# Sixteen blocks of the down projections as seven products, with left operands made in the up phase

## The chip, the cores and the metric

One core of a Trainium2 chip runs the kernel. The time is that of one execution on the device, in microseconds (us); of several executions the median counts.

## What is computed

One decoder layer on x (1024 tokens, 1024 channels, float32): a feed-forward block, a mixer, a second feed-forward block. The change is in the two feed-forward blocks (FFN1 and FFN2), which have D_FF = 2816 channels:

```python
def swiglu(x, w_gate, w_up, w_down):
    return (jax.nn.silu(x @ w_gate) * (x @ w_up)) @ w_down
...
        f = swiglu(rmsnorm(x, ffn1_pre_g[l]), ffn1_w_gate[l], ffn1_w_up[l], ffn1_w_down[l])
        x = x + 0.5 * rmsnorm(f, ffn1_post_g[l])
```

## The kernel before

Every float32 product is made of three matmuls on high and low parts, `mm3` (L118 to L121: high x high, high x low, low x high), each 128 x 128 x 512. A high part is a rounded copy, a low part is the original minus it. The 2816 channels are 22 blocks `f` of 128. Tokens are 8 tiles `tt` of 128 or 2 halves `h` of 512.

**Up phase** (`Ffn.up`, L395). For each block, gate and up projection. Blocks 0 and 1 are plain; blocks 2 to 21 use a block form in which seven products of quarter matrices, combined with additions, stand for eight (`product`, L368). Products go in the order 1, 2, 5, 6, 4, 7, 3 into the PSUM banks X, Z, DY, DW; ACT copies partial sums out of a bank that a later product accumulates over (L374, L378, L382), DVE adds the rest (L383 to L390). `prep` (L291) makes the weights' operands for the next block: four DVE combinations (L297 to L300), seven high parts (four on POOL, L307; three on ACT, L305), seven low parts on POOL (L308). The operands are 512 elements wide; `slot` (L280) takes them from pool `fu` or `WP`, two halves to a tile. SP loads the weights two blocks ahead (`load`, L270). The block's result h goes to DRAM by ACT's queue (`put`, L347).

**Down phase** (`ffn_down`, L420). Blocks in four chunks `CH` of 6, 6, 6 and 4. For each chunk, output half n and token tile tt: SP loads h of the chunk from DRAM (L431), ACT makes the high part (L433), DVE the low part (L435), PE runs 3 matmuls for each block, ACT copies the bank (L452, first chunk) or DVE adds it to the sum `acc` (L454). Weights come 2 blocks x 512 columns at a time through `weight` (L93): SP loads 512 KB, POOL makes high and low part (L107, L108). After the last chunk `post` normalises and adds the residual.

Each engine runs its instructions in one fixed order, the order of the program text (SP's, ACT's and POOL's transfers included); a transfer waits in its engine's queue like any instruction. Pools of tiles with a fixed number of buffers decide how far an engine runs ahead.

## Time and profile before

| | us |
|---|---|
| median of 3 runs | 2267.06 (2266.55 to 2268.98) |
| profiled execution, whole time | 2267.87 |
| its span | 2266.1 |
| TensorE busy in it | 2142.8 (95%) |
| FFN1: up products, down | about 106 to 487, 487 to 737 |
| FFN2: up products, down | about 1630 to 2009, 2013 to 2258 |

The span is the time from the first to the last instruction; 1.77 us of the profiled execution lie outside it. The granted clock of the profiled execution is 0.97 on the mean. Rows of the profile name engine (PE is TensorE, DVE VectorE, ACT ScalarE, POOL GpSimd, SP the queue that issues most transfers), line, operation, output tile and input tiles, and shape.

### The profile page before, as it was taken

The page shows a single profiled execution, that of the slowest core. Times are in us where ns is not written, and L with a number is a line of the kernel's source. Part 1 is how long each engine was busy: PE and PEld are TensorE (multiplying, and loading weights), DVE is VectorE, ACT ScalarE, POOL GpSimd, SP SyncE. Part 2 cuts the span into 40 slices and gives each one's busy share as a digit, 9 for nine tenths or more (in the row PEclk, how much of TensorE's full clock was granted, in tenths as well). Part 3 has the DMA queues.
Part 4 walks back from the last instruction along what each step waited for, and adds up shares of the span by engine and source line. Part 5 has one row for each costly group of instructions (what it writes and reads, how often), then busy time and mean ns, then how long its engine had stood idle before and what let it go on. Part 6 is the DMA issues. An engine that isn't in the chain of part 4 may idle for free.

```text
span 2266.1 us, 29554 instructions
## 1 busy us (share of the span) xinstructions
PE 2142.8 (95%) x11168; PEld 1764.5 (78%) x11168; DVE 1102.3 (49%) x1652; ACT 786.0 (35%) x1349; POOL 963.7 (43%) x875
## 2 busy tenths in 40 slices
PE   7799999999999999999999999899799999999998
PEld 5678888878887777777888887777678888878886
DVE  4743333322445555735617778636743333322446
...
GB/s 116 70 93 91 75 90 75 67 142 183 142 149 130 93 164 119 109 168 99 229 161 117 187 200 108 130 139 121 76 91 84 84 84 84 66 137 169 130 135 162
DMA packets 295277, 276.16 MB, mean 122 GB/s; under 512 B 29664, under 2 KB 237536, under 8 KB 295136
## 3 DMA queue, kind: packets, MB, share of 16 engines
...
q14 instruction: 53, 0.43, 0.1%
HBM read 195.60 MB, written 78.64 MB: 121 GB/s over the span
## 4 chain that ended last, share of the span: by engine, by line
PE 78%; DVE 10%; POOL 4%; ACT 4%; issue 3%; DMA 1%; SPq 0%; DVEq 0%; ACTq 0%; POOLq 0%
PE f1d L120 3%; PE f1d L121 3%; PE f1d L119 3%; PE pj L119 3%; PE f2d L119 3%; PE f2d L120 3%; PE f2d L121 3%; PE pj L121 3%; PE pj L120 3%; PE f2X L119 2%; PE f2X L120 2%; PE f2X L121 2%; PE f1X L119 2%; PE f1X L121 2%; PE f1X L120 2%
## 5 line engine op out<-in xcount | busy, mean ns | idle before, releaser
L107 POOL TENSOR_SCALAR wh<-wr 128x1024 fp32r<-128x1024 f32 x87 | 112.1, 1289 | 480.3 <-PE f1d L121 152.8
L108 POOL TENSOR_TENSOR wl<-wr,wh 128x1024 fp32r<-128x1024 f32 x87 | 213.5, 2455 | 6.0 <-PE pj L121 0.2
L120 PE MATMUL f1d<-wl,f1hh 128*128 128x512 f32 x352 | 138.8, 394 | 3.9 <-POOL wl L108 3.9
L119 PE MATMUL f2d<-wh,f2hh 128*128 128x512 f32 x352 | 137.9, 392 | 4.7 <-issue 3.5
L121 PE MATMUL f1d<-wh,f1hl 128*128 128x512 f32 x352 | 138.6, 394 | 0.4 <-DVE f1hl L435 0.4
L119 PE MATMUL f1d<-wh,f1hh 128*128 128x512 f32 x352 | 138.1, 393 | 0.0
L120 PE MATMUL f2d<-wl,f2hh 128*128 128x512 f32 x352 | 137.7, 391 | 0.0
L121 PE MATMUL f2d<-wh,f2hl 128*128 128x512 f32 x352 | 137.4, 390 | 0.0
L308 POOL TENSOR_TENSOR f2wl<-f2S,f2wh 128x512 fp32r<-128x512 f32 x80 | 104.0, 1311 | 4.0 <-ACT f2wh L305 1.7
L308 POOL TENSOR_TENSOR f1wl<-f1S,f1wh 128x512 fp32r<-128x512 f32 x80 | 103.9, 1310 | 4.0 <-ACT f1wh L305 1.7
L433 ACT CAST f2hh<-f2r 128x768 fp32r<-128x768 f32 (+1 forms) x56 | 45.1, 808 | 165.8 <-PE f2d L120 109.1
L433 ACT CAST f1hh<-f1r 128x768 fp32r<-128x768 f32 (+1 forms) x56 | 45.1, 807 | 165.7 <-PE f1d L120 109.8
L435 DVE TENSOR_TENSOR f2hl<-f2r,f2hh 128x768 fp32r<-128x768 f32 (+1 forms) x56 | 55.8, 998 | 68.9 <-ACT f2hh L433 68.9
L435 DVE TENSOR_TENSOR f1hl<-f1r,f1hh 128x768 fp32r<-128x768 f32 (+1 forms) x56 | 56.5, 1008 | 66.5 <-ACT f1hh L433 66.5
L308 POOL TENSOR_TENSOR f2wl<-f2r,f2wh 128x512 fp32r<-128x512 f32 x60 | 86.0, 1440 | 2.3
L308 POOL TENSOR_TENSOR f1wl<-f1r,f1wh 128x512 fp32r<-128x512 f32 x60 | 85.9, 1439 | 2.3
L307 POOL TENSOR_SCALAR f1wh<-f1r 128x512 fp32r<-128x512 f32 x40 | 33.4, 837 | 114.8 <-DMA f1r<-in_ffn_w_gate_dram 60.3
L119 PEld LDWEIGHTS f2d<-wh,f2hh 128*128 128x128 f32 x352 | 66.4, 189 | 19.6 <-issue 3.9
L120 PEld LDWEIGHTS f1d<-wl,f1hh 128*128 128x128 f32 x352 | 66.9, 190 | 18.5 <-POOL wl L108 4.7
L121 PEld LDWEIGHTS f1d<-wh,f1hl 128*128 128x128 f32 x352 | 66.9, 190 | 14.7 <-DVE f1hl L435 0.8
L119 PEld LDWEIGHTS f1d<-wh,f1hh 128*128 128x128 f32 x352 | 66.8, 190 | 14.0
L307 POOL TENSOR_SCALAR f2wh<-f2r 128x512 fp32r<-128x512 f32 x40 | 33.4, 835 | 104.0 <-DMA f2r<-in_ffn_w_gate_dram 49.5
...
## 6 DMA issues: line engine op xcount, KB each, us to landing
wr<-in_ffn_w_down_dram SPq DMA_DIRECT2D x44, 512.0 KB, 3.9
f1r<-f1h_d SPq DMA_DIRECT2D x48, 384.0 KB, 3.5
f2r<-f2h_d SPq DMA_DIRECT2D x48, 384.0 KB, 3.5
wr<-in_w_in_dram SPq DMA_DIRECT2D x27, 512.0 KB, 4.0
f1r<-in_ffn_w_gate_dram SPq DMA_DIRECT2D x20, 512.0 KB, 3.9
f1r<-in_ffn_w_up_dram SPq DMA_DIRECT2D x20, 512.0 KB, 4.0
f2r<-in_ffn_w_gate_dram SPq DMA_DIRECT2D x20, 512.0 KB, 3.9
f2r<-in_ffn_w_up_dram SPq DMA_DIRECT2D x20, 512.0 KB, 3.9
```

The costliest lines, as they stand in the source:

```text
L107: nc.gpsimd.tensor_scalar(wh, raw, 1.0, 0.0, op0=ALU.mult, op1=ALU.add)
L108: nc.gpsimd.tensor_tensor(wl, raw, wh, op=ALU.subtract)
L119: nc.tensor.matmul(ps, lhsT=lh, rhs=rh, start=first, stop=False, **kw)
L120: nc.tensor.matmul(ps, lhsT=lh, rhs=rl, start=False, stop=False, **kw)
L121: nc.tensor.matmul(ps, lhsT=ll, rhs=rh, start=False, stop=last, **kw)
L307: nc.gpsimd.tensor_scalar(wh, src[n], 1.0, 0.0, op0=ALU.mult, op1=ALU.add)
L308: nc.gpsimd.tensor_tensor(wl, src[n], wh, op=ALU.subtract)
L433: nc.scalar.copy(hh, raw)
L435: nc.vector.tensor_tensor(hl, raw, hh, op=ALU.subtract)
```

## The change

The up phase now also makes the down projection's left operands. `split_pair` takes two neighbouring blocks' h (`hv`), makes the seven combinations that the block form needs, splits each into high (ACT) and low (DVE), and stores both with SP (256 KB each); its seven pieces are called by `split_step` between the matmul groups of the next even block's `product`. The plain blocks 0, 1 and 18 to 21 are split without combining. The results are in three DRAM tiles `hf` (blocks 0, 1), `hs` (2 to 17) and `hl` (18 to 21). The pools of the up phase change: S 2 to 1 tiles, wh and wl 2 to 1, tp 8 to 6, new are hv 2 and st 6.

The down phase starts with blocks 0 and 1 (plain, six matmuls per bank), goes on with four groups `c` of four blocks in the seven-product form, each with 4 steps `i` of two token tiles (42 matmuls, seven additions by DVE), and ends with blocks 18 to 21 (plain). `prep(c + 1)` stands at the first step of group c: four weight loads, four DVE combinations (128x1024), seven high parts on ACT, seven low parts on POOL. Left operands come from DRAM ready to use, once.

```diff
-    CH = [(0, 6), (6, 6), (12, 6), (18, 4)]
+    NS, FS, FL = 4, 2, 18
...
+            self.hf = dr.tile([NT, P, 2, 2, P], F32, name=f"{nm}hf_d")
+            self.hs = dr.tile([NS, 4, 8, P, 2, 2, P], F32, name=f"{nm}hs_d")
+            self.hl = dr.tile([NT, 2, P, 4, P], F32, name=f"{nm}hl_d")
...
-                pool = self.fu if i % 6 < 2 else WP
+                pool = self.fu if i % 5 < 1 else WP
...
             src = {1: A11, 2: A12, 5: S1, 6: S2, 4: A22, 7: S3, 3: S4}
             for n in PO:
+                if n == 3:
+                    tt(S4, A12, S2, op=ALU.subtract)
                 wh, wl = self.slot()
...
+            t = WP.tile("wr", f"{self.nm}es{f}_{h}", [P, 1024], F32R)
+            self.split(hv, t[:, 0:HT], t[:, HT:], lambda x: self.hf[4 * h:4 * h + 4, :, x, f, :])
...
+        def split(self, src, hi, lo, dst):
+            nc.scalar.copy(hi, src)
+            nc.vector.tensor_tensor(lo, src, hi, op=ALU.subtract)
+            for x, t in enumerate((hi, lo)):
+                nc.sync.dma_start(dst(x).rearrange("i p t -> p i t"),
+                                  t.bitcast(F32).rearrange("p (i t) -> p i t", t=P))
...
+        def split_pair(self, f):
+            v = [self.hv.pop(x).rearrange("p (i b t) -> p b i t", b=2, t=P) for x in (f, f + 1)]
+            A11, A21, A12, A22 = v[0][:, 0], v[0][:, 1], v[1][:, 0], v[1][:, 1]
+            c, k = divmod(f - FS, 4)
+            v3 = lambda t: t.rearrange("p (i t) -> p i t", t=P)
+            tt = nc.vector.tensor_tensor
+            def out_(n, src):
+                hi, lo = self.st("sh"), self.st("sl")
+                nc.scalar.copy(v3(hi), src)
+                tt(v3(lo), src, v3(hi), op=ALU.subtract)
+                for x, t in enumerate((hi, lo)):
+                    nc.sync.dma_start(self.hs[c, :, n, :, x, k // 2, :].rearrange("i p t -> p i t"),
+                                      v3(t.bitcast(F32)))
+            out_(1, A11)
+            yield
+            out_(2, A12)
+            yield
+            s1 = v3(self.st("s1", F32))
+            tt(s1, A21, A22, op=ALU.add)
+            out_(5, s1)
+            yield
+            s2 = v3(self.st("s2", F32))
+            tt(s2, s1, A11, op=ALU.subtract)
+            out_(6, s2)
+            yield
+            out_(4, A22)
+            yield
+            tt(s1, A11, A21, op=ALU.subtract)
+            out_(7, s1)
+            yield
+            tt(s2, A12, s2, op=ALU.subtract)
+            out_(3, s2)
...
         def product(self, f):
             self.mm(f, 1, "X")
+            self.split_step()
             self.mm(f, 2, "Z")
+            self.split_step()
             self.evac1(f)
             y = self.mm(f, 5, "DY")
             y5 = self.tile(f, "y")
             nc.scalar.copy(y5, y)
-            self.store(f - 1)
+            self.split_step()
             x = self.mm(f, 6, "X", False)
             u2 = self.tile(f, "u")
             nc.scalar.copy(u2, x)
+            self.split_step()
             w = self.mm(f, 4, "DW")
+            self.split_step()
...
+            h = self.hv[f] = self.fu.tile("hv", f"{self.nm}hv{f}", [P, T])
+            nc.vector.tensor_tensor(h[:, 0:HT], p1, u3, op=ALU.mult)
+            nc.vector.tensor_tensor(h[:, HT:T], u2, y5, op=ALU.mult)
+            if f >= FL:
+                self.sp.append(self.split_plain(f))
+            elif (f - FS) % 2:
+                self.sp.append(self.split_pair(f - 1))
...
-            self.fu = Pool(self.nm + "u", dict(raw=2, S=2, wh=2, wl=2, tp=8))
+            self.fu = Pool(self.nm + "u", dict(raw=2, S=1, wh=1, wl=1, tp=6, hv=2, st=6))
...
+        rp = Pool(nm + "rp", dict(wh=6, wl=6, rw=5, T=2), "right")
...
+        def slot():
+            i = nslot[0]
+            nslot[0] += 1
+            pool = rp if i % 10 < 6 else WP
+            return [v2(pool.tile(t, f"{nm}d{t}{i}", [P, 1024], F32R)) for t in ("wh", "wl")]
+        def prep(c):
+            f0 = FS + 4 * c
+            first = slot()
+            B = {}
+            for kh, e in ((0, 0), (0, 1), (1, 1), (1, 0)):
+                B[kh, e] = v2(rp.tile("rw", f"{nm}B{c}{kh}{e}", [P, 1024]))
+                nc.sync.dma_start(B[kh, e], F.wd[:, f0 + kh:f0 + kh + 4:2, e * 512:(e + 1) * 512])
+            T1, T2 = [v2(rp.tile("T", f"{nm}T{c}{i}", [P, 1024])) for i in range(2)]
+            tt = nc.vector.tensor_tensor
+            tt(T1, B[0, 1], B[0, 0], op=ALU.subtract)
+            tt(T2, B[1, 1], T1, op=ALU.subtract)
+            src = {1: B[0, 0], 2: B[1, 0], 5: T1, 6: T2, 3: B[1, 1], 7: B[0, 1], 4: B[1, 0]}
+            for n in (1, 2, 5, 6, 3, 7, 4):
+                if n == 7:
+                    tt(B[0, 1], B[1, 1], B[0, 1], op=ALU.subtract)
+                if n == 4:
+                    tt(B[1, 0], B[1, 0], T2, op=ALU.subtract)
+                wh, wl = first or slot()
+                first = None
+                nc.scalar.copy(wh, src[n])
+                nc.gpsimd.tensor_tensor(wl, src[n], wh, op=ALU.subtract)
+                op[c, n] = wh, wl
...
+        W = [weight(F.wd[:, 0:2, n * 512:(n + 1) * 512], 2, 512, False) for n in range(2)]
+        prep(0)
+        for tt in range(NT):
+            h2 = pl.tile("ho", f"{nm}hf{tt}", [P, 2, 2, P], F32R)
+            nc.sync.dma_start(h2.bitcast(F32), F.hf[tt])
+            for n in range(2):
+                ps = bank("A", f"{nm}df{n}_{tt}")
+                for i in range(2):
+                    mm3(ps, h2[:, 0, i, :], h2[:, 1, i, :], W[n][0][:, i, :], W[n][1][:, i, :], i == 0, i == 1)
+                nc.scalar.copy(quarter(tt, n), ps)
...
+        for s_, (c, i) in enumerate(steps):
+            if i == 0 and c + 1 < NS:
+                prep(c + 1)
+            if s_ + 1 < len(steps):
+                hos[steps[s_ + 1]] = hload(*steps[s_ + 1])
+            ho = hos.pop((c, i))
+            a_, b_ = 2 * i, 2 * i + 1
+            X = bank("A", f"{nm}dX{c}{i}")
+            mm(c, ho, 1, X, True)
+            add(a_, 0, X)
+            if late is not None:
+                late()
+            Z = bank("D", f"{nm}dZ{c}{i}")
+            mm(c, ho, 2, Z, True)
+            add(a_, 0, Z)
+            Y = bank("mm", f"{nm}dY{c}{i}")
+            mm(c, ho, 5, Y, True)
+            add(b_, 1, Y)
+            mm(c, ho, 6, X, False)
+            add(a_, 1, X)
+            mm(c, ho, 3, Y, False)
+            add(a_, 1, Y)
+            mm(c, ho, 7, X, False)
+            add(b_, 1, X)
+            def late(c=c, ho=ho, X=X, b_=b_):
+                mm(c, ho, 4, X, False)
+                add(b_, 0, X)
```

Three places in the order of the engines follow. The first is ACT in the up phase at block 8 of FFN1, in the kernel before: `p8`, `y8`, `u8`, `v8` are copies of banks, `wh` weight operands.

```order
L357 COPY f1p8_1568<-f1X8_1542 128x512
L305 CAST f1wh_27_1532<-f1S9_1_1513 128x512
L359 ACTIVATE f1p8_1568<-f1p8_1568 128x512
L374 COPY f1y8_1585<-f1DY8_1572 128x512
L305 CAST f1wh_28_1654<-f1r0_10_1538 128x512
L378 COPY f1u8_1601<-f1X8_1542 128x512
L305 CAST f1wh_29_1660<-f1S10_0_1648 128x512
L382 COPY f1v8_1628<-f1X8_1542 128x512
L387 ACTIVATE f1u8_1601<-f1u8_1601 128x512
```

After it stands:

```order
L451 ACTIVATE f1u7_1564<-f1u7_1564 128x512
L382 CAST f1sh35_1673<-f1hv7_1609 128x512
L421 COPY f1p8_1679<-f1X8_1641 128x512
L382 CAST f1sh38_1700<-f1s137_1698 128x512
L311 CAST f1wh_26_1624<-f1S9_1612 128x512
L423 ACTIVATE f1p8_1679<-f1p8_1679 128x512
L382 CAST f1sh41_1722<-f1s240_1720 128x512
L434 COPY f1y8_1696<-f1DY8_1683 128x512
L382 CAST f1sh43_1741<-f1hv7_1609 128x512
L382 CAST f1sh45_1764<-f1s137_1698 128x512
L311 CAST f1wh_27_1630<-f1r1_9_1505 128x512
L438 COPY f1u8_1718<-f1X8_1641 128x512
```

The casts of L382 (`sh`, the high parts of the combinations of blocks 6 and 7) stand among the copies; between `p8` and `u8` there are four of them.

The second is SP at the end of the up phase of FFN1, before (`wr` down weights, `r0` the chunk's h, the operand of the first down matmuls):

```order
L276 DMA f1r1_21_3048<-in_ffn1_w_up_dram 128x8x128
L104 DMA wr4_3418<-in_ffn1_w_down_dram 128x2x512
L104 DMA wr5_3424<-in_ffn1_w_down_dram 128x2x512
L104 DMA wr6_3430<-in_ffn1_w_down_dram 128x2x512
L104 DMA wr7_3652<-in_ffn1_w_down_dram 128x2x512
L431 DMA f1r0_0_3412<-f1h_d0_120 128x768
```

And after (`ph`, `pl` the parts of block 21's h; `B` weights of the first seven-product group; `hf0` the left operand of the first down matmuls):

```order
L513 DMA f1B000_3838<-in_ffn1_w_down_dram 128x2x512
L359 DMA f1hl_d_122<-f1ph141_3791 128x4x128
L359 DMA f1hl_d_122<-f1pl142_3792 128x4x128
L359 DMA f1hl_d_122<-f1ph143_3797 128x4x128
L359 DMA f1hl_d_122<-f1pl144_3798 128x4x128
L513 DMA f1B001_3840<-in_ffn1_w_down_dram 128x2x512
L513 DMA f1B011_3842<-in_ffn1_w_down_dram 128x2x512
L513 DMA f1B010_3844<-in_ffn1_w_down_dram 128x2x512
L542 DMA f1hf0_3878<-f1hf_d_120 128x512
L542 DMA f1hf1_3896<-f1hf_d_120 128x512
```

The loads of h stand behind the stores of block 21 and three more loads of weights.

The third is DVE in FFN1's down phase, before, in the second chunk (`f1hl` low parts of h, `f1d` banks):

```order
L454 TENSOR_TENSOR f1acc0_3455<-f1d1_0_0_3896,f1acc0_3455 128x512
L435 TENSOR_TENSOR f1hl1_3_3972<-f1r1_3_3968,f1hh1_3_3970 128x768
L454 TENSOR_TENSOR f1acc1_3482<-f1d1_0_1_3922,f1acc1_3482 128x512
L435 TENSOR_TENSOR f1hl1_4_3998<-f1r1_4_3994,f1hh1_4_3996 128x768
L454 TENSOR_TENSOR f1acc2_3509<-f1d1_0_2_3948,f1acc2_3509 128x512
L435 TENSOR_TENSOR f1hl1_5_4024<-f1r1_5_4020,f1hh1_5_4022 128x768
```

After, where the first step of group 1 begins (`dX03` and `dY03` are banks of the last step of group 0, `dX10`, `dZ10`, `dY10` of this one; `T2` and `B2` are combinations for group 2):

```order
L499 TENSOR_TENSOR f1acc6_3819<-f1dY03_4306,f1acc6_3819 128x512
L499 TENSOR_TENSOR f1acc7_3820<-f1dX03_4283,f1acc7_3820 128x512
L517 TENSOR_TENSOR f1T21_4346<-f1B211_4341,f1T20_4345 128x1024
L521 TENSOR_TENSOR f1B201_4339<-f1B211_4341,f1B201_4339 128x1024
L499 TENSOR_TENSOR f1acc0_3813<-f1dX10_4391,f1acc0_3813 128x512
L499 TENSOR_TENSOR f1acc7_3820<-f1dX03_4283,f1acc7_3820 128x512
L523 TENSOR_TENSOR f1B210_4343<-f1B210_4343,f1T21_4346 128x1024
L499 TENSOR_TENSOR f1acc0_3813<-f1dZ10_4406,f1acc0_3813 128x512
L499 TENSOR_TENSOR f1acc1_3814<-f1dY10_4414,f1acc1_3814 128x512
```

Three combinations for the next group but one stand before the addition that empties `dY10`.

## Rows read from the trace of the kernel before

**Rows 1.** The page: busy time by engine, and the chain that ended last.
```profile
PE 2142.8 (95%) x11168; PEld 1764.5 (78%) x11168; DVE 1102.3 (49%) x1652; ACT 786.0 (35%) x1349; POOL 963.7 (43%) x875
...
PE 78%; DVE 10%; POOL 4%; ACT 4%; issue 3%; DMA 1%; SPq 0%; DVEq 0%; ACTq 0%; POOLq 0%
```

**Rows 2.** Two stretches: busy us (instructions) of PE, PEld, DVE, ACT, POOL; clock, DMA, GB/s.
```profile
130.00:480.00 350.00, 348.24 (x1537) 288.03 (x1536) 131.08 (x180) 97.09 (x165) 209.62 (x195) 1.00 0.29 82
480.00:500.00 20.00, 17.59 (x70) 13.64 (x69) 8.20 (x9) 4.91 (x8) 11.46 (x6) 0.91 0.63 198
```

**Rows 3.** The page's costliest groups: busy, mean ns, idle before.
```profile
L108 POOL TENSOR_TENSOR wl<-wr,wh 128x1024 fp32r<-128x1024 f32 x87 | 213.5, 2455 | 6.0 <-PE pj L121 0.2
L120 PE MATMUL f1d<-wl,f1hh 128*128 128x512 f32 x352 | 138.8, 394 | 3.9 <-POOL wl L108 3.9
```

**Rows 4.** Timeline, POOL and DVE, 287 to 291 us: start, length, instruction, [idle before].
```profile
287.02 1.29 POOL L308 TENSOR_TENSOR f1wl<-f1S,f1wh 128x512 fp32r<-128x512 f32 x1
288.27 1.29 POOL L308 TENSOR_TENSOR f1wl<-f1r,f1wh 128x512 fp32r<-128x512 f32 x1
...
288.34 1.76 DVE L299 TENSOR_TENSOR f1S<-f1r,f1r 128x512 f32<-128x512 f32 x1 [4.29 <-POOL f1wl L308]
```

**Rows 5.** Groups by line and shape, 130 to 480 us, POOL, DVE and ACT.
```profile
L308 POOL TENSOR_TENSOR f1wl<-f1S,f1wh 128x512 fp32r<-128x512 f32 x70 | 90.4, 1301 | 3.9 <-ACT f1wh L305 1.7
L307 POOL TENSOR_SCALAR f1wh<-f1S 128x512 fp32r<-128x512 f32 x35 | 21.9, 627 | 64.9 <-PE f1Z L120 19.1 <-PE f1X L120 17.4 <-PE f1DW L120 14.9
...
L390 DVE TENSOR_TENSOR f1y<-f1u,f1y 128x512 f32<-128x512 f32 x19 | 17.5, 919 | 1.4 <-ACT f1u L387 1.4
...
L305 ACT CAST f1wh<-f1S 128x512 fp32r<-128x512 f32 x35 | 21.8, 623 | 58.6 <-PE f1X L120 34.8 <-PE f1DY L120 17.7 <-PE f1X L121 3.4
L378 ACT COPY f1u<-f1X 128x512 f32<-128x512 f32 x19 | 11.1, 586 | 22.0 <-PE f1X L121 22.0
```

**Rows 6.** Timeline, POOL, at the start of FFN1's up products.
```profile
85.67 7.43 POOL L307 TENSOR_SCALAR f1wh<-f1r 128x512 fp32r<-128x512 f32 x1 [60.34 <-DMA f1r<-in_ffn_w_gate_dram]
```

**Rows 7.** Timeline, PE and DVE, from FFN1's last up matmul on.
```profile
486.87 0.39 PE L121 MATMUL f1DY<-X_1h,f1wl 128*128 128x512 f32 x1
487.10 0.39 PE L119 MATMUL f1d<-wh,f1hh 128*128 128x512 f32 x1
...
489.51 0.50 PE L121 MATMUL f1d<-wh,f1hl 128*128 128x512 f32 x1 [0.42 <-DVE f1hl L435]
...
493.17 0.50 PE L120 MATMUL f1d<-wl,f1hh 128*128 128x512 f32 x1 [1.99 <-POOL wl L108]
...
495.46 0.63 PE L119 MATMUL f1d<-wh,f1hh 128*128 128x512 f32 x1
495.89 0.63 PE L120 MATMUL f1d<-wl,f1hh 128*128 128x512 f32 x1
...
487.30 0.69 DVE L386 TENSOR_TENSOR f1u<-f1DY,f1u 128x512 f32<-128x512 f32 x1
...
489.37 1.53 DVE L390 TENSOR_TENSOR f1y<-f1u,f1y 128x512 f32<-128x512 f32 x1
```

**Rows 8.** Timeline, PE, from FFN2's last up matmul on.
```profile
2008.90 0.39 PE L121 MATMUL f2DY<-x2X4h,f2wl 128*128 128x512 f32 x1
2012.83 0.47 PE L119 MATMUL f2d<-wh,f2hh 128*128 128x512 f32 x1 [3.54 <-issue]
```

**Rows 9.** DMA issues: count, KB each, median us to landing.
```profile
wr<-in_ffn_w_down_dram SPq DMA_DIRECT2D x44, 512.0 KB, 3.9
f1r<-f1h_d SPq DMA_DIRECT2D x48, 384.0 KB, 3.5
...
f1r<-f1h_d SPq DMA_DIRECT2D x8, 256.0 KB, 2.6
```

**Rows 10.** Groups by line and shape, DVE, 500 to 730 us.
```profile
L454 DVE TENSOR_TENSOR f1acc<-f1d,f1acc 128x512 f32<-128x512 f32 x45 | 31.0, 690 | 71.8 <-PE f1d L121 71.5
L496 DVE TENSOR_TENSOR f1acc<-f1acc,gpost 128x1024 f32<-128x1024 f32 x5 | 6.1, 1220 | 1.3 <-ACT x1q0j L480 0.7 <-ACT x1q1j L480 0.6
```

More of the change, by code (lines that the diff above doesn't have):

```diff
@@ L292, in prep @@
             G, U = self.raw.pop(f)
-            S = [self.fu.tile("S", f"{self.nm}S{f}_{i}", [P, 1024]) for i in range(2)]
-            S1, S2, S3, S4 = [self.half(S[i // 2], i % 2) for i in range(4)]
+            S = self.fu.tile("S", f"{self.nm}S{f}", [P, 1024])
+            S1, S2 = [self.half(S, i) for i in range(2)]
             A11, A12, A21, A22 = G[:, 0:4], G[:, 4:8], U[:, 0:4], U[:, 4:8]
+            S3, S4 = A21, A12
             tt = nc.vector.tensor_tensor
@@ new lines, in split_plain @@
+        def split_plain(self, f):
+            t = self.hv.pop(f)
+            for h in range(2):
+                self.split(t[:, h * HT:(h + 1) * HT], self.st("ph"), self.st("pl"),
+                           lambda x: self.hl[4 * h:4 * h + 4, x, :, f - FL, :])
+                yield
[28 more added lines that the diff above has]
+            out_(7, s1)
+            yield
+            tt(s2, A12, s2, op=ALU.subtract)
+            out_(3, s2)
@@ L352, in tile, with split_step @@
+        def split_step(self):
+            while self.sp:
+                try:
+                    next(self.sp[0])
+                    return
+                except StopIteration:
+                    self.sp.pop(0)
         def tile(self, f, n):
@@ L360, in evac1 @@
             self.tp[f] = p1
-        def store(self, f):
-            if f not in self.tp:
-                return
-            for h, t in enumerate(self.tp.pop(f)):
-                self.put(f, h, t)
         def product(self, f):
             self.mm(f, 1, "X")
+            self.split_step()
             self.mm(f, 2, "Z")
+            self.split_step()
             self.evac1(f)
@@ L416, in up, with ffn_down @@
                 self.product(f)
[L417 removed]
+            while self.sp:
+                self.split_step()
             self.fu.close()
[L420 removed]
+    def ffn_down(pl, F, gb, post, half=None, nextx=None):
         nm = F.nm
[L422 to L469 removed]
@@ new lines, in ffn_down, with add @@
+        acc = [pl.t4(f"{nm}acc{tt}") for tt in range(NT)]
+        rp = Pool(nm + "rp", dict(wh=6, wl=6, rw=5, T=2), "right")
+        quarter = lambda tt, n: acc[tt][:, n * 512:(n + 1) * 512]
+        v2 = lambda t: t.rearrange("p (k e) -> p k e", k=2)
+        nslot = [0]
+        op = {}
+        def add(tt, n, ps):
+            nc.vector.tensor_tensor(quarter(tt, n), ps, quarter(tt, n), op=ALU.add)
+        def slot():
[3 more added lines that the diff above has]
+            return [v2(pool.tile(t, f"{nm}d{t}{i}", [P, 1024], F32R)) for t in ("wh", "wl")]
@@ new lines, in ffn_down, with mm @@
+        steps = [(c, i) for c in range(NS) for i in range(4)]
+        hos = {steps[0]: hload(*steps[0])}
+        late = None
+        def mm(c, ho, n, ps, first):
+            wh, wl = op[c, n]
+            for k in range(2):
+                mm3(ps, ho[n][:, 0, k, :], ho[n][:, 1, k, :], wh[:, k, :], wl[:, k, :], first and k == 0, k == 1,
+                    skip_group_check=True)
+        for s_, (c, i) in enumerate(steps):
[25 more added lines that the diff above has]
+                add(b_, 0, X)
@@ new lines, in ffn_down @@
+        late()
+        rp.close()
+        if nextx is not None:
+            nextx()
+        ex = EX[0] = Pool(nm + "ex", dict(wh=2, wl=2), "right")
+        gb[0] = gb[0]()
+        W = {}
+        for tt in range(NT):
+            hh, hl = [pl.tile("ho", f"{nm}hl{x}{tt}", [P, 4, P], F32R) for x in range(2)]
+            for x, t in enumerate((hh, hl)):
+                nc.sync.dma_start(t.bitcast(F32), F.hl[tt, x])
+            for n in range(2):
+                ps = bank("A", f"{nm}dl{n}_{tt}")
+                for i in range(4):
+                    if (n, i // 2) not in W:
+                        W[n, i // 2] = weight(F.wd[:, FL + i:FL + i + 2, n * 512:(n + 1) * 512], 2, 512, i == 2)
+                    dh, dl = W[n, i // 2]
+                    mm3(ps, hh[:, i, :], hl[:, i, :], dh[:, i % 2, :], dl[:, i % 2, :], i == 0, i == 3)
+                add(tt, n, ps)
+                if half is not None and tt == NT - 1:
+                    half(n, acc[tt])
+            if half is None or tt < NT - 1:
+                post(tt, acc[tt])
@@ L1390, in layer_kernel @@
     PS.open("psf2d", FP)
-    HP = Pool("h2", HB, "right")
-    pl = EX[0] = Pool("f2", dict(FB, t4=20, t2=4))
+    pl = Pool("f2", dict(FB, t2=4))
     gb = [lambda: bcast(pl, "gpost2", a["ffn2_post_g"], 0.5)]
-    ffn_down(pl, HP, F2, gb, *make_last(pl, "x3", x2_d, gb, out[0]))
+    ffn_down(pl, F2, gb, *make_last(pl, "x3", x2_d, gb, out[0]))
     pl.close()
-    HP.close()
     WP.close()
```

85 lines of the change are left out of this document (20 added, 65 removed).

## The prediction

> **What bounds the kernel now.** I read the share of busy time and the chain of waits first: TensorE is busy 2142.8 of the 2266.1 us span and carries 78% of the chain [rows 1]. Then the stretches, to see where that is literally so. From 130 to 480 us, the seven-product part of the first FFN's up phase, PE is busy 348.24 of 350 us at full granted clock while POOL is busy only 209.62 and DVE 131.08 [rows 2]. The second FFN runs the same code. The down projection between 500 and 736 us is as dense, apart from a few waits on POOL's low parts of weights. So a removed matmul is worth its full slot, and each new wait of PE costs its full length. In the profile PE idles round the FFNs only at three places: the start of the up products, the hand-over from up to down, and the last chunk's first weights. The question for this change is whether the engines off the path stay off it, because it gives DVE, ACT and SP more to do and takes buffers from POOL.
>
> **1. Matmuls removed.** One down projection is 22 blocks x 8 token tiles x 2 halves x 3 = 1056 matmuls, 352 by each of three lines [rows 3]. Sixteen blocks in seven products instead of eight leave 4 groups x 4 token pairs x 42 = 672, and six plain blocks 288: 960, so 96 fewer per FFN and 192 in all. A slot is 348.24 / 1537 = 0.2266 us [rows 2]. 192 x 0.2266 = **-43.5 us** over both FFNs, with nothing else in its way. A product of six matmuls lasts 1.36 us and a step of 42 lasts 9.52; an up product of 84 lasts 19.04.
>
> **2. The up phase gets work on DVE, ACT and SP.** The split of h moves here from the down phase. Every second block (f = 4, 6 ... 18: eight per FFN) now carries seven casts on ACT, eleven 128x512 operations on DVE and fourteen stores on SP; I call it a heavy block. ACT has room: 97 of 350 us [rows 2], and seven casts of 0.62 more in 19 us. DVE looks idle as well (37%), but it does not run freely beside POOL. At 288.34 the add of L299 had waited 4.29 us for POOL and then took 1.76 us instead of 0.69, and it finished only when POOL's two subtractions of 1.29 us were done [rows 4]. L390 averages 0.919 over the stretch for the same reason [rows 5]. So for DVE operations that read two SBUF operands the two engines are one resource. The Trainium skill says so too ("SBUF — State Buffer", section "SBUF: two separate sides"): such a DVE operation and a GpSimd operation that reads SBUF take a lock for their whole length, and the second blocks. The wait of 4.29 agrees; it is the rule that speaks against this change, since by it the extra time on DVE is paid in POOL's time, and without it the term below would be nought.
>
> What this resource holds per block: POOL does four high parts of 0.63 and seven low parts of 1.30 [rows 5], 11.6 us; DVE does six two-operand operations of 0.69 (one at [rows 7]), 4.1 us: 15.7 of 19.04. A heavy block adds eleven operations at some 0.62 each, 6.8 us: 22.5 of 19.04, an excess of 3.5, where its light neighbour has 3.3 to spare. Over a pair the load is 38.2 of 38.1 us: just full. What decides is how far POOL can work ahead, and the change shrinks its operand slots from 12 half tiles to 10 and the temporaries (tp) from 8 to 6. The place where PE would notice is the copy `u` of the fourth product (L378 before, 0.586 us and right behind its product [rows 5]): the sixth product overwrites that bank. The order of ACT puts three stores' casts and one weight cast ahead of it, each fed by DVE in its turn. Going through one heavy block by hand, with those durations and the lock, `u` ends 1.5 us after its product could have gone on; without the lock it is in time. Bounds per heavy block: 0 (POOL ahead, excess carried into the light block) and 3.5 (nothing carried). I take 1.2, nearer to the first because the pair as a whole just fits: 16 x 1.2 = **+19.2 us** (0 to 56).
>
> **3. Start of the up products.** In both, DVE's 128x2048 operations hold POOL off: one high part of 128x512 lasted 7.43 us there instead of 0.63 [rows 6]. After the change the gate weights of block 2 stand on SP behind the last plain store, whose subtraction stands on DVE behind the last of the long operations, so they leave later; but by then DVE's long operations are done and POOL no longer starves. The products' start comes out where it is: **0** (-2 to +4 per FFN).
>
> **4. Hand-over from up to down.** Before, the first down operands (chunk 0 of h) were loaded and split long ahead: in the first FFN the first down matmul follows the last up matmul in 0.23 us, and all waits there sum to 0.2 + 0.42 + 1.99 us [rows 7]; in the second the gap is 2012.83 - 2008.90 = 3.9 us [rows 8]. After the change SP has, in this order: one weight load, the four stores of block 21's halves, three more 512 KB weight loads for the seven-product group, and only then `hf0`, the first down matmul's left operand. The stores need block 21's h. On the clock of the first FFN: DVE's adds begin at 487.30 and the last multiplication starts at 488.7 when POOL is quiet (it was 489.37 [rows 7]); cast, subtraction and two more follow, so the first store issues at about 489.4, the last at 490.8, and `hf0` at about 492.2. Alone, a 256 KB load lands in 2.6 us [rows 9]: 494.8, 7.8 us after the last up matmul. But 1 MB of stores and 1.5 MB of loads were issued just ahead of it. 384 KB lands in 3.5 and 512 KB in 3.9 us [rows 9], so another 128 KB takes some 0.4 us, and 2.75 MB takes 8.6 us from 489.4: 498, or 11 us. At the 198 GB/s of the stretch 480 to 500 [rows 2] it would be 16. The Trainium skill ("DMA: Bandwidth & Descriptors", section "Queues, rings and completion order") states that descriptors on each ring are consumed in ring order; by that `hf0` stands behind all of it and 11 is right, while 7.8 needs it to overtake. No row shows which. I take 11.3 us: +8.9 in the first FFN (against 2.4), +7.4 in the second (against 3.9): **+16.3 us** (9.3 to 26). The slow matmuls behind such a gap were there before: after the 1.99 us wait eight follow at 0.43 us apart, and the stretch's granted clock is 0.91, that is, part of it at 1.2 instead of 2.4 GHz [rows 2, 7].
>
> **5. The seven-product down phase.** PE takes a step of 9.52 us, in which DVE makes seven PSUM additions of 0.69 us [rows 10], 4.8 us: enough room on the average. But the weights' combinations of the next group stand among these additions in DVE's fixed order. At the first step of group 1 the combination `B210` is two additions ahead of the one that frees bank Y. It needs POOL's low part of the second product of group 2, and POOL reaches that only after six low parts of 2.455 us [rows 3], the first of which must wait for its slot until the last step of group 0 is under way. From that step's start: PE wants bank Y free at 16.5 us; POOL's six operations, the first at 2.5, the others back to back or at their slots, end at 17.4; then 1.22 us for `B210` [rows 10] and two additions give 20.0, or 21.7 with the lock and the cast between. I take 4 (bounds 2.8 and 6). The same stands at the start of group 2; at that of group 3 nothing is prepared. At the start of group 0 a combination waits for a slot that the plain blocks hold: 2 us (0 to 3). Together 10 us per FFN. The two long stalls are over the 1.99 us after which PE was slow for eight matmuls, 8 x 0.2 = 1.6 us each: 3.2. So 13.2 per FFN, **+26.4 us** (11 to 40). The reloads, casts and subtractions of h that this phase loses (56 each per FFN before) were hidden; taking them away gives nothing.
>
> **Sum.** -43.5 + 19.2 + 0 + 16.3 + 26.4 = +18.4 us. The profiled execution took 2267.87 us (1.77 round its span), 0.8 above the median of 2267.06; from the median the forecast is 2285.5 us. About 0.2%, 4.5 us, is what a measurement here can tell from no change.
>
> **Rivals.**
> - *Cover holds, the change pays*: POOL and DVE carry the excess over into the light blocks, no `u` comes late, `hf0` overtakes, and the down stalls are at their lower bounds: -43.5 + 0 + 9.3 + 11.2 = -23, and with middling hand-over and stalls -43.5 + 16 + 16 = -11: 2244 to 2258. For it: POOL is busy only 60% of the stretch [rows 2], and the waits of DVE were harmless. Against it: the lock, the smaller pools, and DVE's order, which is fixed.
> - *Nothing is carried over*: each heavy block stalls for 3 us or more, and PE's clock falls after each, another 1.6: 16 x 4.6 = 74 instead of 19 gives 2340; with half of them so, 2313. For it: the pair's load is just full. Against it: ACT and SP have room, and only one bank's copy is in the way.
> - *The stalls cancel the gain*: heavy blocks at 0.3 us and the rest as above: 2271, no change.
>
> **Chances.** The forecast's own case (2268 to 2300) 0.45; the change pays 0.35; nothing carried over 0.15; the rest beyond either. Faster by over 0.2% 0.36, within 0.2% 0.11, slower by over 0.2% 0.53. Range 2245 to 2318: it leaves out the lowest bounds together and the worst case of the heavy blocks.
>
> **What would show it.** In the profile after: the PE stretch 130 to 480 should lose about 1.2 us at every second product, PE waiting for ACT's `u` copy; if PE is as dense as before there, step 2 is wrong and the time falls below 2270. Between the last up and the first down matmul there should be about 11 us of idle PE, waiting for a DMA of `hf`. At two places about 40 us apart in each down phase PE should wait some 4 us for a DVE addition out of bank Y, with DVE waiting for POOL. If these waits are short, step 5 is wrong. If the down phase's steps themselves exceed 9.52 us, I have missed a load or a copy.

## The result and the profile after

The changed kernel takes 2328.61 us (median of 4 runs, 2326.29 to 2329.67) against 2268.02 for the kernel before on the same chip: a ratio of **1.0266, 95% interval 1.0248 to 1.0284**. It is slower by 60.6 us, more than three times the forecast's +18.4, and 10.6 us above the upper end of the range.

The page's busy times and chain [rows 1] now read:

```profile
PE 2124.4 (91%) x10976; PEld 1740.6 (75%) x10976; DVE 1359.3 (58%) x1932; ACT 825.0 (35%) x1429; POOL 1007.6 (43%) x867
...
PE 64%; DVE 15%; issue 6%; ACT 5%; POOL 5%; DMA 3%; SPq 0%; DVEq 0%; ACTq 0%; POOLq 0%
```

192 matmuls fewer, yet PE's share of the chain fell from 78% to 64%, and DVE's rose from 10% to 15%. What PE waits for in the two FFNs (us in all, times, longest):

```profile
PE f2X L119 <- ACT f2u L438: 14.7, 9, 1.7
PE f1X L119 <- ACT f1u L438: 14.0, 9, 1.7
PE f1X L119 <- POOL f1wh L313: 12.8, 1, 12.8
...
PE f2df L119 <- DMA f2hf<-f2hf_d: 12.3, 1, 12.3
PE f1df L119 <- DMA f1hf<-f1hf_d: 12.2, 1, 12.2
PE f2dY L119 <- issue: 8.0, 2, 4.1
PE f1dY L119 <- issue: 6.0, 2, 3.1
PE f2dX L119 <- issue: 5.2, 2, 2.6
...
PE f1X L119 <- ACT f1p L421: 5.0, 1, 5.0
...
PE f1dX L119 <- DVE f1acc L499: 2.7, 1, 2.7
...
PE f1dX L119 <- ACT f1dwh L526: 2.6, 1, 2.6
```

Three of the places are those that the prediction named: the copy `u` in the heavy blocks, the hand-over, the group starts. The fourth is the start of the up products, which it put at nothing: there PE of FFN1 waits 12.8 us for its first weights and, later, 5.0 us for the copy `p` (6.65 and 1.76 in the kernel before, with 6.8 in two waits between them). By stretches, from the first and last matmul of each:

| stretch | before | after | difference | forecast |
|---|---|---|---|---|
| FFN1, up to its last up matmul | 486.9 | 507.0 | +20.1 | +9.6 |
| FFN1, last up to first down matmul | 0.2 | 12.6 | +12.4 | +11.1 |
| FFN1, down | 249.5 | 247.4 | -2.1 | -10.8 |
| FFN1 down end to FFN2's last up matmul | 1272.3 | 1292.3 | +20.0 | +9.6 |
| FFN2, last up to first down matmul | 3.9 | 12.7 | +8.8 | +7.4 |
| FFN2, down | 242.6 | 244.0 | +1.4 | -8.6 |
| end | 10.7 | 9.7 | -1.0 | 0 |
| span | 2266.1 | 2325.7 | +59.6 | +18.3 |

(The forecast's 2.4 us at FFN1's hand-over holds 2.2 that lie in the down stretch; here they are counted there. The table of the kernel before has the up products begin at about 106 and 1630 us; their first matmuls start at 93.16 and 1615.15.) At the start of FFN1's up products, first in the kernel before, then in the changed one, the profile shows SP, POOL and PE:

```profile
93.16 0.79 PE L119 MATMUL f1X<-X_0h,f1wh 128*128 128x512 f32 x1 [6.65 <-POOL f1wh L307]
```

```profile
94.05 0.46 SPq L280 DMA_DIRECT2D f1r<-in_ffn_w_gate_dram  x1
...
98.83 0.62 POOL L313 TENSOR_SCALAR f1wh<-f1r 128x512 fp32r<-128x512 f32 x1 [73.46 <-DMA f1r<-in_ffn_w_gate_dram]
...
99.51 0.79 PE L119 MATMUL f1X<-X_0h,f1wh 128*128 128x512 f32 x1 [12.80 <-POOL f1wh L313]
```

The first up matmul comes 6.3 us later. The stretches of [rows 2], 130 to 480 us, and the hand-over, columns as there:

```profile
130.00:480.00 350.00, 331.26 (x1443) 271.29 (x1442) 215.39 (x267) 122.83 (x218) 226.68 (x193) 0.99 0.50 140
507.00:513.00 6.00, 0.43 (x2) 0.01 (x1) 3.07 (x5) 2.81 (x4) 1.77 (x1) 0.88 0.64 169
513.00:519.00 6.00, 0.00 (x0) 0.00 (x0) 2.70 (x3) 0.20 (x1) 0.57 (x1) 0.50 1.04 357
```

PE has 331.26 us of work where it had 348.24. Of the 18.7 us without work, 13.7 are the eight waits for `u`; the other 5.0 are the single wait for the copy `p`, at 135.58. In one heavy block, the timeline shows SP, POOL, DVE, ACT and PE:

```profile
239.75 0.36 SPq L385 DMA_DIRECT2D f1hs_d<-f1sh  x1
...
240.22 1.60 POOL L314 TENSOR_TENSOR f1wl<-f1r,f1wh 128x512 fp32r<-128x512 f32 x1
...
240.59 1.78 DVE L383 TENSOR_TENSOR f1sl<-f1s,f1sh 128x512 fp32r<-128x512 f32 x1
...
242.40 0.62 ACT L382 CAST f1sh<-f1s 128x512 fp32r<-128x512 f32 x1 [1.35 <-DVE f1sl L383]
...
243.45 0.58 ACT L438 COPY f1u<-f1X 128x512 f32<-128x512 f32 x1
...
244.08 0.50 PE L119 MATMUL f1X<-X_1h,f1wh 128*128 128x512 f32 x1 [1.72 <-ACT f1u L438]
```

DVE's subtraction takes 1.78 us beside POOL's 1.60 and ends at 242.37. ACT's cast waits 1.35 us for it, `u` leaves only then, PE waits 1.72. The cast has a second condition that ends almost as late: it also waits for the store of an earlier high part, issued at 239.75 and landed 2.4 us later, at 242.16, which frees one of the six store buffers. The next such wait had been at 203.97, so two blocks take 40.11 us instead of 2 x 19.04 = 38.08: 2.0 us lost per heavy block, 16 per FFN.

At the start of group 1 (same views, and one stretch with its granted clock; the four lines of DVE stand one after the other):

```profile
588.12 1.92 DVE L517 TENSOR_TENSOR f1T<-f1B,f1T 128x1024 f32<-128x1024 f32 x1 [1.35 <-DMA f1B<-in_ffn_w_down_dram]
589.96 3.39 DVE L521 TENSOR_TENSOR f1B<-f1B,f1B 128x1024 f32<-128x1024 f32 x1
593.28 1.28 DVE L499 TENSOR_TENSOR f1acc<-f1dX,f1acc 128x512 f32<-128x512 f32 x2
595.61 3.37 DVE L523 TENSOR_TENSOR f1B<-f1B,f1T 128x1024 f32<-128x1024 f32 x1 [1.05 <-POOL f1dwl L527]
...
594.06 0.77 PE L119 MATMUL f1dX<-f1dwh,f1ho 128*128 128x512 f32 x1 [2.58 <-ACT f1dwh L526]
...
600.27 0.75 PE L119 MATMUL f1dY<-f1dwh,f1ho 128*128 128x512 f32 x1 [3.06 <-issue]
...
600.80:603.40 2.60, 2.60 (x8) 2.00 (x7) 0.21 (x1) 0.00 (x0) 0.00 (x0) 0.50 0.02 5
```

Two waits, not one: the addition that empties bank X starts at 593.28, behind the combinations of 1.92 and 3.39 us, and the one for bank Y behind a third of 3.37. (The profile puts the first wait down to ACT, but the matmul starts right after the addition.) Behind the first wait six matmuls, behind the second seven come 0.43 us apart instead of 0.23, at a granted clock of 0.50, that is 1.2 instead of 2.4 GHz.

The order that an engine keeps is fixed, but it is not that of the program text, which it was said to be above: `prep(c + 1)` is written ahead of the whole step, and still DVE's order has the additions of `acc0` and `acc7` ahead of `B210`. So an edit that moves one instruction in the text can move others, too.

### The profile page after: what moved, and what is told of

It reads as the page before. It is cut to its first block, busy times and chain, and to the rows that moved or that the text cites. A ratio compares the mean times of both kernels' runs of the same rounds, so it can differ in the third digit from the quotient of the medians.

```text
span 2325.7 us, 30338 instructions
## 1 busy us (share of the span) xinstructions
PE 2124.4 (91%) x10976; PEld 1740.6 (75%) x10976; DVE 1359.3 (58%) x1932; ACT 825.0 (35%) x1429; POOL 1007.6 (43%) x867
## 4 chain that ended last, share of the span: by engine, by line
PE 64%; DVE 15%; issue 6%; ACT 5%; POOL 5%; DMA 3%; SPq 0%; DVEq 0%; ACTq 0%; POOLq 0%
PE pj L119 3%; PE pj L121 3%; PE pj L120 3%; PE f1X L119 2%; PE f2X L119 2%; PE f1X L121 2%; PE f1X L120 2%; PE f2X L121 2%; PE f2X L120 2%; POOL f2wl L314 1%; PE a_512o L1416 1%; POOL f1wl L314 1%; PE f1DY L120 1%; PE f1DY L119 1%; PE f1dX L119 1%
## 5 line engine op out<-in xcount | busy, mean ns | idle before, releaser
L314 POOL TENSOR_TENSOR f2wl<-f2r,f2wh 128x512 fp32r<-128x512 f32 x100 | 141.2, 1422 | 21.4 <-ACT f2wh L311 18.1
L314 POOL TENSOR_TENSOR f1wl<-f1r,f1wh 128x512 fp32r<-128x512 f32 x100 | 141.1, 1422 | 21.3 <-ACT f1wh L311 18.1
L108 POOL TENSOR_TENSOR wl<-wr,wh 128x1024 fp32r<-128x1024 f32 x55 | 136.9, 2491 | 21.1 <-PE f1dY L121 17.9
L119 PE MATMUL pj<-x1X4h,wh 128*128 128x512 f32 x176 | 76.5, 435 | 0.0
L119 PE MATMUL pj<-x1X2h,wh 128*128 128x512 f32 x176 | 72.6, 413 | 0.6 <-DVE qkl L1106 0.5
L121 PE MATMUL pj<-x1X4h,wl 128*128 128x512 f32 x176 | 72.0, 409 | 0.0
L120 PE MATMUL pj<-x1X4l,wh 128*128 128x512 f32 x176 | 70.6, 401 | 0.0
L121 PE MATMUL pj<-x1X2h,wl 128*128 128x512 f32 x176 | 69.4, 394 | 0.0
L120 PE MATMUL pj<-x1X2l,wh 128*128 128x512 f32 x176 | 69.3, 394 | 0.0
L445 DVE TENSOR_TENSOR f2y<-f2X,f2y 128x512 f32<-128x512 f32 x20 | 13.8, 691 | 89.7 <-ACT f2v L444 89.3
L445 DVE TENSOR_TENSOR f1y<-f1X,f1y 128x512 f32<-128x512 f32 x20 | 13.8, 691 | 88.9 <-ACT f1v L444 88.5
L527 POOL TENSOR_TENSOR f1dwl<-f1B,f1dwh 128x1024 fp32r<-128x1024 f32 x20 | 53.0, 2676 | 24.1 <-ACT f1dwh L526 24.1
L527 POOL TENSOR_TENSOR f2dwl<-f2B,f2dwh 128x1024 fp32r<-128x1024 f32 x20 | 52.3, 2644 | 24.7 <-ACT f2dwh L526 24.7
```

Of the source, the lines that this page charges most:

```text
L108: nc.gpsimd.tensor_tensor(wl, raw, wh, op=ALU.subtract)
L119: nc.tensor.matmul(ps, lhsT=lh, rhs=rh, start=first, stop=False, **kw)
L120: nc.tensor.matmul(ps, lhsT=lh, rhs=rl, start=False, stop=False, **kw)
L121: nc.tensor.matmul(ps, lhsT=ll, rhs=rh, start=False, stop=last, **kw)
L314: nc.gpsimd.tensor_tensor(wl, src[n], wh, op=ALU.subtract)
L445: nc.vector.tensor_tensor(y5, x, y5, op=ALU.add)
```

## The experiments

Theory: the block form is worth its 43.5 us, and **orders and a shared resource** take it away: fixed places in the queues of ACT, DVE and SP, with DVE's two-operand operations and POOL excluding one another. Rivals: the engines' time as such is too much (DVE and POOL over-full, POOL's low parts too slow, too many bytes). Each kernel ran once, beside the kernel before on the same chip, and differs from the changed kernel by what is named; e12 is the median of five runs. Single runs of the kernel before differ by up to 0.4% on one chip (2265.65 to 2274.19), so small differences of ratios say nothing, and the stretches and waits of the traces carry the argument. The changed kernel's ratio is 1.0266.

| run | ratio to before | FFN1: up products, gap, down (us) |
|---|---|---|
| before / changed | 1 / 1.0266 | 393.7, 0.2, 249.5 / 407.5, 12.6, 247.4 |
| e1 hf on ACT's queue | 1.0324 | 408.6, 5.8, 258.5 |
| e2 no low parts of combinations | 1.0129 | 391.8, 12.9, 249.0 |
| e3 spread over two blocks | 1.0135 | 391.7, 12.3, 246.5 |
| e4 no combinations of weights | 1.0028 | 408.1, 12.1, 223.2 |
| e5 `u` copy first | 1.0109 | 393.8, 12.6, 248.9 |
| e6 combinations behind a step | 1.0115 | 408.7, 12.1, 233.6 |
| e7 hf before weights on SP | 1.0280 | 407.9, 7.6, 258.8 |
| e8 low parts on POOL | 1.0674 | 452.5, 12.4, 248.4 |
| e9 three orders | 0.9895 | 391.9, 12.5, 224.2 |
| e10 and weights' order | 0.9915 | 391.9, 12.5, 224.3 |
| e11 and mixed loads | 0.9893 | 391.8, 7.7, 229.5 |
| e12 as e9, five rounds | 0.9865 (0.9846 to 0.9883) | 391.1, 12.4, 223.9 |

### The heavy blocks

**e2: seven of eleven DVE operations taken out.**

```diff
-                hi, lo = self.st("sh"), self.st("sl")
+                hi = self.st("sh")
...
-                tt(v3(lo), src, v3(hi), op=ALU.subtract)
-                for x, t in enumerate((hi, lo)):
+                for x, t in enumerate((hi, hi)):
```

> split_pair leaves out its seven DVE subtractions and stores the high part twice: seven of eleven DVE operations fewer in every heavy block, while casts on ACT, stores on SP and bytes stay. The low parts of the left operands of blocks 2 to 17 are thus left out. Theory (DVE and POOL share one resource, and DVE's lateness holds up the casts ahead of the u copy): the waits of 1.72 us for the u copy vanish at all 16 heavy blocks, about 32 us less in all. Rival (the casts wait for store buffers and SP): the waits stay within 0.5 us of 1.72, under 8 us gained.

From 130 us to the last up matmul, no wait for `u` is left; the up phase is 15.7 us shorter in FFN1. It is not SP, whose fourteen stores stayed. But the edit takes away two things at once: DVE's subtractions and the seven store buffers of the low parts. In the changed kernel the last cast of a high part ahead of `u` waits for both: in the sixteen heavy blocks an earlier store landed 0.2 to 0.3 us before the subtraction ended. So e2 does not tell DVE's lateness from the number of buffers; no run took away one alone.

**e5: the same work in another order of ACT.**

```diff
-            nc.scalar.copy(u2, x)
-            self.split_step()
+            uc = nc.scalar.copy(u2, x).ins
+            with tc.issue_after(uc):
+                self.split_step()
...
```

> Only ACT's order changes: in the heavy blocks the casts of the combinations 6, 4, 7 and 3 are queued behind the copy of u, which stood behind three of them; the work of every engine stays. Theory A (one late copy in a fixed order is what PE waits for): the sixteen waits of 1.72 us go, 25 to 32 us less in all. Theory B (DVE and POOL together are over-full, 38.2 of 38.1 us per pair): the wait moves to another copy or to POOL's operands and under 12 us are gained.

Theory A. What PE waits for from 130 us on is down from

```profile
PE f1X L119 <- ACT f1u L438: 13.7, 8, 1.7
PE f1X L119 <- ACT f1p L421: 5.0, 1, 5.0
```

to the one at the start and two tenths:

```profile
PE f1X L119 <- ACT f1p L421: 5.2, 2, 5.0
```

DVE, POOL and the buffers have the same work as before; the pair of blocks does hold it, though by my count it was just full. So the place of `u` in ACT's order is the cause of PE's wait, whatever made the casts late.

**e3: two of the seven combinations moved to the odd block.**

```diff
+            self.split_out(f, 1, v[:, 0])
...
+            nc.vector.tensor_tensor(s7, v[:, 0], v[:, 1], op=ALU.subtract)
+            self.split_out(f, 7, s7)
...
```

> Two of the seven combinations (1 and 7, which need only the lower block of the pair) are made in the odd block instead of the even one, so that a heavy block has eight DVE operations, five casts and ten stores more instead of eleven, seven and fourteen, and its neighbour three, two and four. The computation is the same. Theory (excess over the block's 19.04 us decides): excess falls from 3.5 to some 1.6 us, the neighbour takes 1.9; the waits for u fall to 0 to 0.5 us, 24 to 32 us less. Rival (the pair as a whole is over-full, DVE plus POOL): the lost time moves to the odd blocks and the sum falls by less than 8 us.

The waits are gone as well, 15.8 us in FFN1's up phase; nothing shows up in the odd blocks.

**e8: the resource that DVE and POOL share.**

```diff
-                tt(v3(lo), src, v3(hi), op=ALU.subtract)
+                nc.gpsimd.tensor_tensor(v3(lo), src, v3(hi), op=ALU.subtract)
```

> The seven subtractions of split_pair run on POOL (1.30 us each) instead of DVE (0.69 us); all else stays, the computation too. Theory (DVE's two-operand operations and POOL share one resource): a heavy block then needs 15.7 + 4 x 0.62 + 7 x 1.30 = 27.3 of 19.04 us and PE loses 5 to 8 us per heavy block, 50 to 100 us more in all. Rival (they run side by side, and only DVE's order was late): POOL needs 20.7 of 19.04 us in a heavy block and 11.6 in the next, the time stays within 15 us of the changed kernel's.

DVE got lighter, and the up phase 45 us longer per FFN: 7.6 us per heavy block in all (452.5 against the 391.8 of e2 and e3, which have no waits), where the excess of 27.3 over 19.04 would be 8.3. The waits from 130 us on, and the last cast of a high part ahead of one `u`:

```profile
PE f1X L119 <- ACT f1u L438: 41.5, 8, 5.8
...
306.36 0.62 ACT L382 CAST f1sh<-f1s 128x512 fp32r<-128x512 f32 x1 [3.32 <-POOL f1sl L383]
```

The rival as it was put (within 15 us of the changed kernel) is out, and the exclusion of [rows 4] fits as a budget. Here it is not shown to be the only cause: the subtractions now also stand in POOL's fixed order, among the weights' parts, the casts wait for POOL there, and side by side POOL would have had 20.7 us of work in a heavy block of 19.04, too. What shows the exclusion itself is the length of single operations: 1.78 us beside POOL instead of 0.68.

### The group starts

**e4: combinations left out.** Products 5, 6, 7 and 4 use uncombined weights.

```diff
-            tt(T1, B[0, 1], B[0, 0], op=ALU.subtract)
-            tt(T2, B[1, 1], T1, op=ALU.subtract)
...
```

> The four DVE combinations of down weights per group are left out (products 5, 6, 7 and 4 use raw weights); loads, casts and POOL's low parts stay. Theory (these operations stand in front of the additions that empty X and Y): the two waits at the start of groups 1 and 2 (2.6 and 3 to 4 us) and the one of 2.7 at the start of group 0 vanish with the slow matmuls behind them, about 20 us per FFN, 40 in all. Rival (POOL's low parts come too late themselves): PE waits for POOL at the same places and under 15 us are gained in all.

The only wait of PE left in FFN1's down phase is that at the hand-over; the phase takes 223.2 us, in FFN2 219.3. So the combinations on DVE cost 24.2 and 24.7 us, and POOL's low parts, which stayed (but no longer wait for a combination), cost nothing.

**e6: combinations kept, behind the additions of the first step.**

```diff
+                with tc.issue_after(behind):
+                    return nc.vector.tensor_tensor(*a, **k)
...
-            if i == 0 and c + 1 < NS:
-                prep(c + 1)
+            if i == 1 and c + 1 < NS:
+                prep(c + 1, last[0])
```

> Only DVE's order in the down phase changes: the weight combinations for the next group are queued behind the last addition of the first step of the group, where POOL has finished its low parts, instead of among the additions; they are still made. Theory (position among the additions, and the 3.4 us that each takes against POOL's low parts): nearly all of what leaving them out gave, 18 to 24 us per FFN, and the combinations take 1.2 us each instead of 3.4. Rival (DVE's time itself, or the loads behind): under 10 us per FFN.

13.8 us of the 24.2 came back, 15.7 in FFN2: less than the theory's 18 to 24, more than the rival's 10. The groups of DVE by line and shape, first of the changed kernel (520 to 720 us), then of e6 (540 to 710):

```profile
L523 DVE TENSOR_TENSOR f1B<-f1B,f1T 128x1024 f32<-128x1024 f32 x4 | 13.5, 3374 | 11.0 <-POOL f1dwl L527 11.0
...
L521 DVE TENSOR_TENSOR f1B<-f1B,f1B 128x1024 f32<-128x1024 f32 x3 | 10.2, 3401 | 0.0
```

```profile
L521 DVE TENSOR_TENSOR f1B<-f1B,f1B 128x1024 f32<-128x1024 f32 x3 | 10.3, 3420 | 0.0
...
L521 DVE TENSOR_TENSOR f1B<-f1B,f1T 128x1024 f32<-128x1024 f32 x3 | 3.6, 1211 | 0.0
```

One of the two locked combinations takes 1.211 us once POOL is quiet; the other, still beside a low part, keeps 3.4, and a row of four holds the next step's additions: PE waits three times 1.75 us for Y.

### The hand-over

**e1, e7 and e11: the loads of hf earlier.** In e1 ACT's queue issues them:

```diff
+        for tt in range(NT):
+            hft.append(pl.tile("ho", f"{nm}hf{tt}", [P, 2, 2, P], F32R))
+            nc.scalar.dma_start(hft[tt].bitcast(F32), F.hf[tt])
         prep(0)
```

> The eight loads of hf (operands of the first down matmuls) are written ahead of the first group's weights and issued by ACT's queue instead of SP's, so that they no longer stand behind three 512 KB loads there. In the changed kernel PE is idle 12.2 and 12.3 us between the last up and the first down matmul. Theory (place in the queue): the gaps fall to 6 to 8 us each, the time by 9 to 12 us. Rival (the transfers of stores and weights fill the DMA engines, whichever queue issues): gaps of 10 us or more, under 4 us gained.

In e7 the loads stay on SP, and the weights are queued behind the second of them:

```diff
+                    with tc.issue_after(hfi[0]):
+                        nc.sync.dma_start(B[kh, e], F.wd[:, f0 + kh:f0 + kh + 4:2, e * 512:(e + 1) * 512])
```

> Only SP's order at the hand-over changes: all loads of hf stand ahead of the four weight loads of the first group, all on SP, and ACT's casts stand behind the first copies. Theory (place in the queue): the gap falls from 12.6 to 6 to 7 us; whether the gain stays depends on the weights, which now come some 4 us later; 8 to 11 us less in all if the plain blocks (22 us) cover them. Rival (the bytes at the hand-over set the time): the wait comes back at the first group's first products, as it did where ACT issued the loads (7.9 us there), and under 3 us are gained.

The place in the queue does set the gap: 12.6 fell to 5.8 and to 7.6 (in e7 all eight loads came to stand ahead of the weights). But FFN1 takes longer from its last up to its last down matmul: 264.3 us in e1 and 266.5 in e7, where the changed kernel takes 260.0. In e1 PE's order changed as well: the second product of the first group (bank Z) came to stand among the plain blocks, and 7 us after the first down matmul PE waits there for its left operand,

```profile
PE f2dZ L119 <- DMA f2ho<-f2hs_d: 8.9, 1, 8.9
PE f1dZ L119 <- DMA f1ho<-f1hs_d: 7.9, 1, 7.9
```

and the first product (bank X) starts 42.3 us after the last up matmul instead of 37.0. In e7 it starts at 37.2, but then PE waits for an addition that stands behind combinations, which came late with the weights:

```profile
PE f1dX L119 <- DVE f1acc L499: 7.3, 2, 6.6
```

e11 put two loads of hf ahead of the weights and the rest between:

```diff
+        hfl(0)
+        hfl(1)
+        for _ in prep(0):
+            pass
+        while len(hft) < NT:
+            hfl(len(hft))
```

> As e10, and at the hand-over SP issues the first two loads of hf ahead of the weights and the rest between and behind them. Theory (POOL's chain decides, not the place of hf alone): the gap falls from 12.5 to 7 or 8 us, and as the weights are behind by only 0.5 to 1 MB, 2 to 4 us of the 5 per FFN stay. Rival (what is gained in the gap is paid at the first group, as in e1 and e7): the sum stays within 3 us of e10 or is above it.

Gap 7.7, down 5.2 us longer than in e10, the product 38.0 us after the last up matmul. There ACT's copies of the plain blocks' banks stand behind the casts of the weights (3.2 us of PE). e11 is 4.9 us faster than e10, but that one had lost 4.4 in FFN2 (below), and 0.45 us faster than e9, less than that scatter. So filling the gap alone gained nothing in three orders, each time for another reason. I read the gap as the visible part of a stretch in which weights, casts, low parts and operands of the first group must all be fetched, at 357 GB/s and a DMA share of 1.04 from 513 to 519 us in the changed kernel; that is not shown. Which of these would have to give to shorten it was not tried.

### Together

**e9, e12**: the spread of e3; the combinations one or two at a time behind steps 0, 1 and 2; the plain blocks' stores by ACT.

```diff
-            self.split(hv, t[:, 0:HT], t[:, HT:], lambda x: self.hf[4 * h:4 * h + 4, :, x, f, :])
+            self.split(hv, t[:, 0:HT], t[:, HT:], lambda x: self.hf[4 * h:4 * h + 4, :, x, f, :], nc.scalar)
...
                 if n == 7:
+                    yield
...
-            if i == 0 and c + 1 < NS:
-                prep(c + 1)
+            if i == 1 and c + 1 < NS:
+                part = prep(c + 1)
+            if i > 0 and c + 1 < NS:
+                next(part, None)
```

> Three edits together, none of which changes the computation: combinations 1 and 7 in the odd block (as in e3); the weight combinations of the next group queued one or two at a time behind the last additions of the steps 0, 1 and 2 of the group, instead of all behind step 0 as in e6; the plain blocks' stores (f = 0, 1) issued by ACT, so that SP has block 2's weight loads ahead of them. Theory: up phase about 392 us from its first matmul as in e3, and that first matmul comes 3 to 6 us earlier than in e3 (100.6) because the gate weights of block 2 no longer wait behind a store; down phase 226 to 230 us (233.6 in e6, 223.1 without the combinations); in all 2255 to 2266. Rival for the start (DVE's long operations hold POOL anyway): the first matmul comes earlier but the following blocks wait, nothing gained there.

> The kernel of e9 again, timed in rounds beside the kernel before. Theory: the orders and not the block form cost the time, so the same 192 matmuls less show as a gain: ratio to the kernel before 0.988 to 0.991 (2240 to 2247 us). Rival (the single look was lucky): 0.995 or more.

Both came out better than expected: e9 at 2242.89 us against 2255 to 2266, e12 at 0.9865 against 0.988 to 0.991. The down phase reaches 223.9, what it takes without the combinations. The start of the up products is 3.6 us earlier in e9 than in e3 (97.0 against 100.6), and the last up matmul 3.4: behind the stores on SP there *was* a cost. It is still 3.9 us later than in the kernel before (93.16); why was not tried. In e12 PE is as dense as in [rows 2]:

```profile
130.00:480.00 350.00, 349.92 (x1544) 289.40 (x1543) 237.10 (x271) 126.83 (x227) 242.49 (x198) 1.00 0.53 146
525.00:677.00 152.00, 152.00 (x672) 125.64 (x671) 89.03 (x123) 20.05 (x19) 61.38 (x29) 1.00 0.77 239
```

This version beats the kernel before, 2239.89 against 2271.33 us or 1.35% less, and with it the changed kernel, which was 2.66% above.

**e10** loaded B10 second:

```diff
-        LOADS = ((0, 0), (0, 1), (1, 1), (1, 0))
+        LOADS = ((0, 0), (1, 0), (0, 1), (1, 1))
```

> As e9, and the four weight loads of a group in the order B00, B10, B01, B11 (the second product needs B10, which came last). Theory (in the first group POOL's chain of seven low parts from the weights' landing decides when the first seven-product step can go on): POOL's second low part starts some 3 us earlier (it stood idle from 513.6 to 519.9 us in the changed kernel), and PE's wait of 2.7 us at the first step of group 0 shrinks by 2 us or more: 2 to 6 us in all. Rival (the additions stand behind a combination there anyway): within 2 us of e9.

A miss: 4.5 us longer than e9, 4.4 of it in FFN2's down phase, where ACT's copies, behind casts that wait for combinations, made the plain blocks wait (2.9 us). The wait it was to shrink had already gone with the orders of e9.

## Why the prediction was wrong

The direction held, though the prediction gave it a chance of no more than 0.53, and so did the mechanisms that it named; the terms of the up phase and of the group starts were too small, all in one direction.

- **1, matmuls.** Right: with the waits of the group starts removed (e4, e9) FFN1's down phase is 25 to 26 us shorter and FFN2's 22 to 23, 21.8 of them the matmuls and the rest waits that the kernel before had itself.
- **2, heavy blocks.** The place was right (e5), the size was not. The hand count gave a stall of 1.5, the trace shows 1.72 and 2.0 with what follows it; I took 1.2 because the pair as a whole just fits. That argument failed: a fixed order cannot use slack that lies elsewhere. 32 us instead of 19.2, both FFNs together; e5 and e3 show that the pair does fit. Of the reasons why the casts come late, DVE beside POOL was named; the six store buffers, which free up at nearly the same time, were not, and the runs do not part the two. The row read as support for the lock was partly misread: the wait of 4.29 in [rows 4] ends when POOL's subtraction that reads the buffer `f1S` ends, and DVE's operation writes that buffer. Only its length, 1.76 instead of 0.69, shows the exclusion.
- **3, start.** Wrong: 0 was taken, with a bound of +4 per FFN, and the first up matmul comes 6.3 us later in FFN1. As forecast, POOL is no longer held up (its first part takes 0.62 us instead of 7.43), but the gate weights leave SP only at 94.05, and POOL has them at 98.83; this time to landing was left out. The up phases lost 40.1 us; take off the 32, and 4 us net per FFN are left, of which moving the stores gave 3.4 back in FFN1 (e9 against e3). The 5.0 us wait for `p` stayed open.
- **4, hand-over.** Nearly right: a gap of 11.3 was forecast, 12.6 and 12.7 measured. That three other orders of the loads gained nothing (e1, e7, e11) was unforeseen.
- **5, group starts.** The step that failed most: 13.2 us per FFN forecast, 24.2 and 24.7 measured (e4); the down phases moved by -0.7 instead of -43.5 together. I looked for the one late addition, that of Y, and took one wait of 4. The rows of DVE's order that I quoted show two more combinations ahead of the addition that empties X, and each that meets POOL runs at 3.4 us, where I charged 1.22 or a part. So there are two waits at groups 1 and 2: 2.6 us for X, which was in no term, and 2.9 to 4.1 for Y, about what was taken; with 2.7 and 0.4 to 0.7 at group 0 they come to 14.2 us in FFN1 and 16.5 in FFN2. Most of the rest is PE's slow matmuls, behind more waits than the two that I counted.
- **The range** left the upper ends out as unlikely together. They were not independent: the heavy blocks and the group starts share the same lock and the same habit, a ready instruction placed ahead of an urgent one.
